# Differential attention in a two-layer block: scores on two row halves, one division less, nine steps beside the value products

## The chip, the cores and the metric

The program runs on one core of a Trainium2 chip. The metric is device time in microseconds for one execution: the median of three runs before the change. TensorE is called PE in the rows, VectorE DVE, ScalarE ACT, GpSimd POOL and SyncE SP; SP issues the transfers from HBM.

## The reference, cut to what matters

One transformer block of two layers is followed by a second one with a mixture of experts; the change touches the attention of the first block's second layer alone. There are 256 latent tokens and 256 context tokens, eight heads, and two components of 64 dimensions in each head:

```python
def diff_attn_core(q, k, v, lam):
    s = jnp.einsum('bqhcd,bkhcd->bhcqk', q, k) * DIFF_HEAD_DIM ** -0.5
    p = jax.nn.softmax(s, axis=-1)
    w = p[:, :, 0] - lam * p[:, :, 1]
    return jnp.einsum('bhqk,bkhe->bqhe', w, v)

def finish(o):
    o = rms_norm(o, subln_gain) * (1.0 - lam_init)
    return o.reshape(b, l, D_MODEL) @ w_out
```

Queries come from the 256 latent tokens, keys and values from all 512. Queries and keys are normalised by group of 64 and rotated before this.

## The kernel before, in words

`diff` first makes queries, keys and values with products of 128 by 128 by 512 in three passes (`mm3`, lines 142 to 144, on a high and a low part of each number). The loop `for i in range(3)` goes over queries, keys and values, `n` over the two halves of the 1024 columns, and `c` over four chunks of weights; a chunk for keys or values is 24 products, into `nj` = 4 accumulators that stay in PSUM for the whole of a half. After a half, ScalarE copies the four accumulators into `vt` (line 1213). `tick` between chunks runs what was put off: normalising, rotating, turning (`turn_qk`, line 1055) and placing the queries and keys. For the scores the queries lie in `qz` twice, with zeros in the rows of the other component, so that one product over 128 rows gives one component.

The attention itself is cut into 16 units u = 2 * head + half of the queries, and written out by hand as a pipeline of steps: `step(t)` issues the scores of unit t (line 1075), the turning of the weights of unit t - 3 (line 1100) with ScalarE's copy of it (line 1101), maxima and exponentials of unit t (lines 1080 and 1087), the weights of unit t - 2 on VectorE (lines 1092 to 1095) and the value products of unit t - 4 (line 1110). The tables `before` and `after` hang the outputs' work on steps: `o_evac` copies the outputs of a group of heads from PSUM, `o_norm` takes squares and the root, `o_scale` divides, `o_turn` (line 1137) turns, `o_split` makes a high and a low part, `out` multiplies by `diff_w_out`. Steps 0 to 3 stand behind the four chunks of the values' second half, the others follow by themselves.

Each engine runs its instructions in the order in which they are written. PSUM has eight buffers, all from one pool (`mm`): four for a half's accumulators, two for a unit's scores, one for a turned block, and in the later steps two for the outputs of a group. A new tile waits until the last reader of the buffer that it gets is done. Six buffers `raw` hold weights on their way in and, two units to a buffer, the exponentials.

Of the kernel before, what the change touches and what calls it, by code (L numbers as in the profile page):

```python
# [9 lines left out]
F32 = mybir.dt.float32  # L10
# [4 lines left out]
AF = mybir.ActivationFunctionType  # L15
OP = mybir.AluOpType
AX = mybir.AxisListType

P = 128
D = 1024  # L20
KD = D // P
L = 256
# [11 lines left out]
EPS = 1e-6  # L34
# [57 lines left out]
class Prog:  # L92
# [791 lines left out]
    def rest(self, cvec):  # L884
        nc, a = self.nc, self.a
# [10 lines left out]
        hh, hl, nx = self.first_norm  # L896

        def first(q):
# [7 lines left out]
        res = lambda layer, piece: lambda k, ps, c: self.add_res(  # L906
            k, ps, ((lat, self.md(layer, 0, piece)),) + (((ctxs, self.md(0, 1, piece)),) if layer == 0 else ()), c)


        lam = self.cp.tile([P, 4], F32, name="lam")  # L910
        subln = self.cp.tile([P, 1], F32, name="subln")
        tabs, norms = [], []
# [48 lines left out]


        kt = self.big([P, KD, T2], F32, "kt")
        qz = self.big([P, KD, 2, L], F32, "qz")
        nc.gpsimd.memset(qz[64:128, :, 0], 0.0)
        nc.gpsimd.memset(qz[0:64, :, 1], 0.0)
        vt = self.big([P, 4, D], F32, "vt")
        hn = self.diff(norms[0], norms[1], kt, qz, vt, tabs[0], tabs[1], lam, subln, res(1, 2))


        self.later(60, self.second_consts)
# [3 lines left out]
        hn = self.hn2 = self.big([P, 2, KD, L], FR, "hn")  # L975
# [35 lines left out]
        nrm.rstd()  # L1011
        nrm.apply()

    def diff(self, hh, hl, kt, qz, vt, tab, gr, lam, subln, res):
        nc, tc = self.nc, self.tc
        w_in = self.a["diff_w_in"]
        qst = self.cp.tile([P, 12, 8], F32, name="qst")
        st = self.cp.tile([P, 16, 8], F32, name="st")
        self.ints = st.rearrange("p a b -> p (a b)").bitcast(I32)
        so = self.so = self.cp.tile([P, 3, 8], F32, name="so")  # L1020
        def stage(n, j):
            return vt[:, j, n * 512:n * 512 + 512]

        def norm(q, n, j):

            r = qst[:, (0, 4)[q] + n * (2, 4)[q] + j]
            x = stage(n, j)
            x8 = x.rearrange("p (g d) -> p g d", g=8)
            sq = self.w(512, "sq")
            nc.scalar.activation(sq, x, AF.Square)  # L1030
            nc.vector.tensor_reduce(r[:, :, None], sq.rearrange("p (g d) -> p g d", g=8), axis=AX.X, op=OP.add)
            nc.scalar.activation(r, r, AF.Sqrt, bias=self.eps, scale=1.0 / 64)
            nc.vector.reciprocal(r, r)
            nc.vector.tensor_tensor(x8, x8, r[:, :, None].to_broadcast([P, 8, 64]), op=OP.mult)
# [17 lines left out]
        def turn_qk(q, n, j):  # L1052
            pt = tp[q, n, j] = self.mm()
            for i in range(4):
                nc.tensor.transpose(pt[:, i * P:i * P + P], stage(n, j)[:, i * P:i * P + P], self.c["ident"])

        def place(q, n, j):
            p4 = tp[q, n, j].rearrange("p (h t) -> p h t", h=4)
            hs, js = slice(4 * n, 4 * n + 4), slice(j * P, j * P + P)
            if q == 1:  # L1060
                nc.scalar.copy(kt[:, hs, js], p4)
            else:
                nc.scalar.copy(qz[0:64, hs, 0, js], p4[0:64])
                nc.scalar.copy(qz[64:128, hs, 1, js], p4[64:128])

        A, po = {}, {}
        groups = ((0, 4), (4, 2), (6, 2))
# [3 lines left out]
        def scores(u):  # L1071
            h, qc = u // 2, u % 2
            A[u, "s"] = [self.mm(), self.mm()]
            for c in range(2):
                nc.tensor.matmul(A[u, "s"][c], qz[:, h, c, qc * P:qc * P + P], kt[:, h], start=True, stop=True)

        def exps(u):
            sm = st[:, u]
            for c in range(2):
                nc.vector.reduce_max(sm[:, c:c + 1], A[u, "s"][c], axis=AX.X)  # L1080
            nc.vector.tensor_scalar(sm[:, 0:2], sm[:, 0:2], -0.125, None, op0=OP.mult)
            if u % 2 == 0:
                A["pw"] = self.raw([P, 2, 2, 512])
            A[u, "p"] = [A["pw"][:, u % 2, c] for c in range(2)]
            A[u, "w"] = A[u, "p"][1]
            for c in range(2):
                nc.scalar.activation(A[u, "p"][c], A[u, "s"][c], AF.Exp, scale=0.125, bias=sm[:, c:c + 1], accum_out=sm[:, 2 + c:3 + c])

        def weights(u):
            sm = st[:, u]  # L1090
            p0, p1 = A[u, "p"]
            nc.vector.reciprocal(sm[:, 4:6], sm[:, 2:4])
            nc.vector.tensor_tensor(sm[:, 6:7], sm[:, 5:6], lam[:, 2:3], op=OP.mult)
            nc.vector.tensor_scalar(p1, p1, sm[:, 6:7], None, op0=OP.mult)
            nc.vector.scalar_tensor_tensor(p0, p0, sm[:, 4:5], p1, op0=OP.mult, op1=OP.add)

        def turn(u):
            pt = self.mm()
            for kc in range(4):
                nc.tensor.transpose(pt[:, kc * P:kc * P + P], A[u, "p"][0][:, kc * P:kc * P + P], self.c["ident"])  # L1100
            nc.scalar.copy(A[u, "w"], pt)

        def values(u):
            h, qc = u // 2, u % 2
            g = group[h]
            i = h - groups[g][0]
            if i == 0:
                po[g, qc] = self.mm()
            for kc in range(4):
                nc.tensor.matmul(po[g, qc][:, i * P:i * P + P], A[u, "w"][:, kc * P:kc * P + P], vt[:, kc, h * P:h * P + P],  # L1110
                                 start=(kc == 0), stop=(kc == 3))
# [4 lines left out]
            nc.scalar.copy(A[g, "o", qc], po[g, qc][:, :n * P])  # L1116

        def o_norm(g):
            n = groups[g][1]
            for qc in range(2):  # L1120
                for i in range(n):
                    nc.scalar.activation(self.junk[:, i * P:i * P + P], A[g, "o", qc][:, i * P:i * P + P], AF.Square,
                                         accum_out=so[:, g, n * qc + i:n * qc + i + 1])
            nc.scalar.activation(so[:, g, :2 * n], so[:, g, :2 * n], AF.Sqrt, bias=self.eps, scale=1.0 / P)

        def o_scale(g):
            n = groups[g][1]
# [36 lines left out]
        b = lambda t, f, *args: before.setdefault(t, []).append((f, args))  # L1164
        e = lambda t, f, *args: after.setdefault(t, []).append((f, args))
        for g, qc, t in ((0, 0, 15), (0, 1, 16), (1, 0, 19), (1, 1, 19)):
            b(t, o_turn, g, qc)
            e(t, o_split, g, qc)
        for g, t in ((0, 11), (1, 15), (2, 19)):
            for qc in range(2):  # L1170
                b(t + qc, o_evac, g, qc)
            e(t + 1, o_norm, g)
            e(t + (3, 2, 1)[g], o_scale, g)
        for t, k in ((16, 0), (17, 1), (18, 2), (19, 3), (20, 4), (20, 5)):
            if k == KD - 3:
                for f in (o_turn, o_split):
# [4 lines left out]
        def step(t):  # L1181
            for f, args in before.get(t, ()):
                f(*args)
            if t < 16:
                scores(t)
            if 0 <= t - 3 < 16:
                turn(t - 3)
            if t < 16:
                exps(t)
            if 0 <= t - 2 < 16:  # L1190
                weights(t - 2)
            if 0 <= t - 4 < 16:
                values(t - 4)
            for f, args in after.get(t, ()):
                f(*args)

        for i in range(3):
            nj = 2 if i == 0 else 4
            for n in range(2):
                pt = [self.mm() for _ in range(nj)]  # L1200
                for c in range(4):
                    wh, wl = self.take()
                    for k in range(2):
                        kk = 2 * c + k
                        s = slice(k * 512, k * 512 + 512)
                        for j in range(nj):
                            js = slice(j * P, j * P + P)
                            self.mm3(pt[j], hh[:, kk, js], hl[:, kk, js], wh[:, s], wl[:, s], kk == 0, kk == KD - 1)
                    self.tick()
                    if i + n == 3:  # L1210
                        step(c)
                for j in range(nj):
                    nc.scalar.copy(stage(n, j), pt[j])
                    if i < 2:
                        at_ = j if i or n else j + 4
                        for d, f in enumerate((norm, rotate, turn_qk, place)):
                            self.later(at_ + d + (2 if i == 0 and n == 1 else 0), f, i, n, j)
        for t in range(4, 21):
            step(t)
        hn = self.big([P, 2, KD, L], FR, "hn")  # L1220
        nrm = self.Norm(self, slice(0, L), self.md(1, 0, 4), self.md(1, 0, 3), hn[:, 0], hn[:, 1])
# [1044 lines left out]
```

## Time and profile before

| | |
|---|---|
| median of three runs | 1411.95 us (1410.03 to 1413.07) |
| profiled execution | 1415.4 us, its span 1413.5 |
| TensorE busy | 1379.9 us, 98% of the span |
| VectorE busy | 780.9 us, 55% |
| ScalarE busy | 535.7 us, 38% |
| GpSimd busy | 8.6 us |
| read from HBM | 372.44 MB, 264 GB/s over the span |
| attention steps on TensorE (line 1075) | first start 575.5, last start 638.0 us |

The span is the time from the first to the last instruction of the program in the profile. Busy shares are means over stages with different limits, so the stage around the change has to be read by itself. A row of TensorE is longer than the distance to the next one, since products follow each other in a pipeline; distances between starts are what a product costs.

### The profile page before, as it was taken

The numbers are of one execution on the slowest core, as the hardware profiler recorded it, in microseconds if no ns is written. First come the engines' busy times: TensorE is split into PE (matmuls) and PEld (weight loads), VectorE is DVE, ScalarE is ACT, GpSimd is POOL, SyncE is SP. The second block draws the span as 40 slices with busy tenths as digits, with TensorE's granted clock in tenths as the row PEclk, the third lists the DMA queues.
The fourth block names the chain that finished last, engine by engine and source line by source line (L and its number), as shares of the span: only waits on it lengthen the run. The fifth ranks groups of instructions, "written<-read, shape, count | busy, mean of one in ns | idle before, by whom it ended". The sixth has DMA issues, their size and how long they took to land. (4 is left out here: it accounts for less than half of the span.)

```text
span 1413.5 us, 20416 instructions
## 1 busy us (share of the span) xinstructions
PE 1379.9 (98%) x8130; PEld 1020.4 (72%) x8130; DVE 780.9 (55%) x1377; ACT 535.7 (38%) x940; POOL 8.6 (1%) x16
## 2 busy tenths in 40 slices
PE   7999999999999999999999999999999999999997
PEld 5789888888889888768899999999543443443442
DVE  5688987778875787496865455676221121121112
ACT  5735322223134555486554345864210111111112
POOL 0000000000001000000000000000000000000000
PEclk9999999999999999999999999999999999999998
DMA  9984754977885531015585544629899999999994
GB/s 365 344 299 151 255 191 144 369 267 267 313 290 169 179 119 60 0 61 179 194 284 179 182 138 150 238 90 398 350 415 422 421 421 421 421 420 422 421 421 179
DMA packets 131426, 374.84 MB, mean 265 GB/s; under 512 B 9457, under 2 KB 63489, under 8 KB 109185
## 3 DMA queue, kind: packets, MB, share of 16 engines
q1 hardware_dynamic: 131328, 373.51, 70.0%
q8 instruction: 65, 1.06, 0.3%
q14 instruction: 33, 0.26, 0.1%
HBM read 372.44 MB, written 1.05 MB: 264 GB/s over the span
## 5 line engine op out<-in xcount | busy, mean ns | idle before, releaser
L133 DVE TENSOR_TENSOR hl<-raw,hl 128x1024 fp32r<-128x1024 f32 (+1 forms) x207 | 250.3, 1218 | 164.3 <-ACT hl L132 164.2
L132 ACT CAST hl<-raw 128x1024 fp32r<-128x1024 f32 (+1 forms) x207 | 213.3, 1044 | 255.4 <-PE mm L144 225.3
L342 DVE SCALAR_TENSOR_TENSOR junk<-raw,cb 128x1024 bf16<-128x1024 f32 x144 | 175.9, 1221 | 2.2
L142 PE MATMUL mm<-hh,hl 128*128 128x512 f32 (+1 forms) x384 | 142.9, 372 | 0.0
L143 PE MATMUL mm<-hl__790,hl 128*128 128x512 f32 (+1 forms) x384 | 142.7, 372 | 0.0
L144 PE MATMUL mm<-hh,hl 128*128 128x512 f32 (+1 forms) x384 | 142.6, 371 | 0.0
L142 PE MATMUL mm<-hn,hl 128*128 128x256 f32 (+1 forms) x488 | 140.2, 287 | 1.1 <-ACT hn L438 1.1
L143 PE MATMUL mm<-hn,hl 128*128 128x256 f32 (+1 forms) x488 | 139.9, 287 | 0.1
L144 PE MATMUL mm<-hn,hl 128*128 128x256 f32 (+1 forms) x488 | 139.2, 285 | 0.0
L142 PE MATMUL mm<-hidh,hl 128*128 128x256 f32 (+1 forms) x400 | 127.1, 318 | 0.0
L143 PE MATMUL mm<-hidl,hl 128*128 128x256 f32 (+1 forms) x400 | 126.7, 317 | 0.0
L144 PE MATMUL mm<-hidh,hl 128*128 128x256 f32 (+1 forms) x400 | 126.7, 317 | 0.0
L1997 PE MATMUL mm<-pre,X 128*64 128x512 f32 x376 | 119.4, 598 | 1.3 <-DMA pre<-in_w_gate 1.3
L1997 PE MATMUL mm<-raw,X 128*64 128x512 f32 x264 | 110.0, 599 | 1.6 <-DMA raw<-in_w_gate 1.3
L142 PEld LDWEIGHTS mm<-hn,hl 128*128 128x128 f32 (+1 forms) x488 | 94.1, 193 | 2.2 <-ACT hn L438 1.3
L2039 DVE SCALAR_TENSOR_TENSOR junk<-mm,rw,x 128x512 f32<-128x512 f32 x29 | 21.8, 752 | 133.7 <-PE mm L2010 131.6
L143 PEld LDWEIGHTS mm<-hn,hl 128*128 128x128 f32 (+1 forms) x488 | 94.1, 193 | 0.9 <-DVE hn L440 0.3
L2112 DVE TENSOR_TENSOR x<-x,mm 128x512 f32<-128x512 f32 x14 | 9.6, 688 | 153.5 <-PE mm L1997 153.5
L144 PEld LDWEIGHTS mm<-hn,hl 128*128 128x128 f32 (+1 forms) x488 | 94.2, 193 | 0.2
L142 PEld LDWEIGHTS mm<-hh,hl 128*128 128x128 f32 x384 | 72.3, 188 | 13.0 <-issue 0.4
L143 PEld LDWEIGHTS mm<-hl__790,hl 128*128 128x128 f32 x384 | 72.3, 188 | 12.6
L144 PEld LDWEIGHTS mm<-hh,hl 128*128 128x128 f32 x384 | 72.3, 188 | 12.4
(449 smaller groups left out, 2498.5 us busy)
## 6 DMA issues: line engine op xcount, KB each, us to landing
raw<-in_adaT SPq DMA_DIRECT2D x56, 1024.0 KB, 6.3
raw<-in_ffn_w_in SPq DMA_DIRECT2D x44, 1024.0 KB, 7.5
pre<-in_w_gate SPq DMA_DIRECT2D x25, 1024.0 KB, 19.7
raw<-in_ffn_w_out SPq DMA_DIRECT2D x22, 1024.0 KB, 5.0
pre<-in_w_up SPq DMA_DIRECT2D x22, 1024.0 KB, 19.8
pre<-in_w_down SPq DMA_DIRECT2D x21, 1024.0 KB, 19.7
raw<-in_w_gate SPq DMA_DIRECT2D x17, 1024.0 KB, 19.7
hl<-in_w_down SPq DMA_DIRECT2D x17, 1024.0 KB, 19.7
```

What stands on the lines that cost most here:

```text
L132: nc.scalar.copy(hi, src)
L133: nc.vector.tensor_tensor(lo, src, hi.bitcast(F32), op=OP.subtract)
L142: nc.tensor.matmul(out, ah, bh, start=start, stop=False)
L143: nc.tensor.matmul(out, ah, bl, start=False, stop=False)
L144: nc.tensor.matmul(out, al, bh, start=False, stop=stop)
L342: nc.vector.scalar_tensor_tensor(self.junk, hold[u][:, j], 1.0, self.cb[layer, s], op0=OP.mult, op1=OP.mult, accum_out=self.mod[layer, s][ ...
L1997: nc.tensor.matmul(St["gu", i][64 * m:64 * m + 64], x_of(k)[:, p % 2 * 2 + (0 if alone(p) else m)], St["w"][m][:, k % 4], start=(k == 0), ...
L2039: nc.vector.scalar_tensor_tensor(k2(t), k2(St["y", n]), self.rw[:, p // 2 % 2, p % 2:p % 2 + 1], gb[:, 2 * n:2 * n + 2], op0=OP.mult, op1= ...
L2112: nc.vector.tensor_tensor(sb, sb, St["gu", 1], op=OP.mult)
```

## The change

Queries are kept once, in `qt`. A unit's scores are four products over 64 rows and 256 columns: component 0 on rows 0 to 63, component 1 on rows 64 to 127, each on its own buffer. The weights are left undivided by the first component's sum: the second component is scaled by lam * sum0 / sum1 and added, and the constant in the output's normalisation is scaled by sum0 squared in its place. The steps beside the products for the values are 0 to 8: step 0 behind the last chunk of the first half, then two behind each chunk of the second half. Value products start at step 9, two units a step until step 13. The copied blocks of the first four units go into the second half of `qt`. The squares of the outputs are one pass with a sum on VectorE, and the first group's outputs are taken at step 13.

```diff
-        qz = self.big([P, KD, 2, L], F32, "qz")
-        nc.gpsimd.memset(qz[64:128, :, 0], 0.0)
-        nc.gpsimd.memset(qz[0:64, :, 1], 0.0)
+        qt = self.big([P, 2, KD, L], F32, "qt")
...
-                nc.scalar.copy(qz[0:64, hs, 0, js], p4[0:64])
-                nc.scalar.copy(qz[64:128, hs, 1, js], p4[64:128])
+                nc.scalar.copy(qt[:, 0, hs, js], p4)
...
-            for c in range(2):
-                nc.tensor.matmul(A[u, "s"][c], qz[:, h, c, qc * P:qc * P + P], kt[:, h], start=True, stop=True)
+            for m in range(2):
+                for c in range(2):
+                    r = slice(64 * c, 64 * c + 64)
+                    ms = slice(m * 256, m * 256 + 256)
+                    nc.tensor.matmul(A[u, "s"][c][:, ms], qt[r, 0, h, qc * P:qc * P + P], kt[r, h, ms], start=True, stop=True)
...
-            A[u, "w"] = A[u, "p"][1]
+            A[u, "w"] = qt[:, 1].rearrange("p h t -> p (h t)")[:, u * 512:u * 512 + 512] if u < 4 else A[u, "p"][1]
...
-            nc.vector.reciprocal(sm[:, 4:6], sm[:, 2:4])
-            nc.vector.tensor_tensor(sm[:, 6:7], sm[:, 5:6], lam[:, 2:3], op=OP.mult)
-            nc.vector.tensor_scalar(p1, p1, sm[:, 6:7], None, op0=OP.mult)
-            nc.vector.scalar_tensor_tensor(p0, p0, sm[:, 4:5], p1, op0=OP.mult, op1=OP.add)
+            nc.vector.reciprocal(sm[:, 4:5], sm[:, 3:4])
+            nc.vector.scalar_tensor_tensor(sm[:, 6:7], sm[:, 4:5], lam[:, 2:3], sm[:, 2:3], op0=OP.mult, op1=OP.mult)
+            nc.vector.scalar_tensor_tensor(p0, p1, sm[:, 6:7], p0, op0=OP.mult, op1=OP.add)
...
             for qc in range(2):
-                for i in range(n):
-                    nc.scalar.activation(self.junk[:, i * P:i * P + P], A[g, "o", qc][:, i * P:i * P + P], AF.Square,
-                                         accum_out=so[:, g, n * qc + i:n * qc + i + 1])
-            nc.scalar.activation(so[:, g, :2 * n], so[:, g, :2 * n], AF.Sqrt, bias=self.eps, scale=1.0 / P)
+                sq = self.w(512, "sq")[:, :n * P]
+                nc.scalar.activation(sq, A[g, "o", qc], AF.Square)
+                r = so[:, g, n * qc:n * qc + n]
+                nc.vector.tensor_reduce(r[:, :, None], sq.rearrange("p (h e) -> p h e", h=n), axis=AX.X, op=OP.add)
+                s0 = st[:, 2 * h0 + qc:2 * h0 + qc + 2 * n - 1:2, 2]
+                e = oe[:, g, n * qc:n * qc + n]
+                nc.vector.scalar_tensor_tensor(e, s0, EPS, s0, op0=OP.mult, op1=OP.mult)
+                nc.vector.scalar_tensor_tensor(r, r, 1.0 / P, e, op0=OP.mult, op1=OP.add)
+            nc.scalar.activation(so[:, g, :2 * n], so[:, g, :2 * n], AF.Sqrt)
...
-        for g, t in ((0, 11), (1, 15), (2, 19)):
+        for g, t in ((0, 13), (1, 15), (2, 19)):
             for qc in range(2):
-                b(t + qc, o_evac, g, qc)
-            e(t + 1, o_norm, g)
-            e(t + (3, 2, 1)[g], o_scale, g)
+                b(t + (g and qc), o_evac, g, qc)
+            e(t + min(g, 1), o_norm, g)
+            e(t + (1, 2, 1)[g], o_scale, g)
...
-            if 0 <= t - 4 < 16:
-                values(t - 4)
+            for u in ((2 * t - 18, 2 * t - 17) if 9 <= t < 14 else (t - 4,) if 14 <= t < 20 else ()):
+                values(u)
...
-                    if i + n == 3:
-                        step(c)
+                    if i == 2:
+                        for t in ((), (), (), (0,), (1, 2), (3, 4), (5, 6), (7, 8))[4 * n + c]:
+                            step(t)
...
-        for t in range(4, 21):
+        for t in range(9, 21):
```

Three places show how the instructions stand. The first is ScalarE's order around the first step; line 1213 before and 1220 now is the copy of a half's four accumulators into `vt`, and the load fetches the table of the exponential. Before:

```order
L1213 COPY vt<-mm 128x512 [waits PE_49] x4
L132 CAST hl<-raw 128x1024 [waits DMAHW2_49]
L1061 COPY kt<-mm 128x4x128 [waits PE_49]
L1087 ACT_TABLE_LOAD
L1087 ACTIVATE raw,st<-mm,st 128x512 [waits DVE_49]
L1087 ACTIVATE raw,st<-mm,st 128x512
L132 CAST hl<-raw 128x1024
```

And now:

```order
L1031 ACTIVATE qst<-qst,eps 128x8 [waits DVE_49]
L1088 ACT_TABLE_LOAD [waits DVE_49]
L1088 ACTIVATE raw,st<-mm,st 128x512 [waits PE_49] x2
L1220 COPY vt<-mm 128x512 x4
L132 CAST hl<-raw 128x1024 [waits DMAHW2_49]
L1060 COPY kt<-mm 128x4x128
L1088 ACTIVATE raw,st<-mm,st 128x512 [waits DVE_49,PE_49]
```

The exponentials of step 0 stand ahead of the copies of the first half, where they stood behind the copies and a conversion of weights; the load of the table stands behind a wait for VectorE, where it waited for nothing.

The second place is TensorE's order behind the last chunk of the values' second half: scores (`mm` from `kt` and `qz`, now `qt`), turned weights (from the unit matrix in `cst`) and value products (from `vt`). Before:

```order
L142 MATMUL mm<-hl,hh 128x512
L143 MATMUL mm<-hl,hh 128x512
L144 MATMUL mm<-hl,hl__3564 128x512
L1075 MATMUL mm<-kt,qz 128x512 x2
L1100 MATMUL mm<-cst,raw 128x128 x4
L1075 MATMUL mm<-kt,qz 128x512 x2
L1100 MATMUL mm<-cst,raw 128x128 x4
L1110 MATMUL mm<-vt,raw 128x128 x4
```

And now:

```order
L142 MATMUL mm<-hl,hh 128x512
L143 MATMUL mm<-hl,hh 128x512
L144 MATMUL mm<-hl,hl__3564 128x512
L1076 MATMUL mm<-kt,qt 128x256 x4
L1100 MATMUL mm<-cst,raw 128x128 x4
L1076 MATMUL mm<-kt,qt 128x256 x4
L1100 MATMUL mm<-cst,raw 128x128 x4
L1076 MATMUL mm<-kt,qt 128x256 x4
L1100 MATMUL mm<-cst,raw 128x128 x4
L1110 MATMUL mm<-vt,qt 128x128 x8
```

Behind a chunk stood one step, and the first step after the last chunk had four value products; now two steps stand behind the chunk, and the first step after the last chunk has eight value products.

The third place is ScalarE's order around the outputs of the first four heads (`o` from PSUM, its squares, the root in `so`). Before:

```order
L1116 COPY o<-mm 128x512 [waits PE_49]
L1101 COPY raw<-mm 128x512 [waits DVE_49,PE_49]
L1087 ACTIVATE raw,st<-mm,st 128x512 [waits DVE_49]
L1087 ACTIVATE raw,st<-mm,st 128x512
L1116 COPY o<-mm 128x512 [waits PE_49]
L1101 COPY raw<-mm 128x512 [waits DVE_49,PE_49]
L1087 ACTIVATE raw,st<-mm,st 128x512 [waits DVE_49,Activation_49]
L1087 ACTIVATE raw,st<-mm,st 128x512
L1122 ACTIVATE junk,so<-o 128x128 [waits Activation_49]
L1122 ACTIVATE junk,so<-o 128x128 x3
L1122 ACTIVATE junk,so<-o 128x128 [waits Activation_49] x4
L1124 ACT_TABLE_LOAD
```

And now:

```order
L1116 COPY o<-mm 128x512 [waits PE_49] x2
L1101 COPY raw<-mm 128x512 [waits DVE_49,PE_49,Activation_49]
L1088 ACTIVATE raw,st<-mm,st 128x512 [waits DVE_49]
L1088 ACTIVATE raw,st<-mm,st 128x512
L1123 ACTIVATE sq<-o 128x512 [waits Activation_49] x2
L1130 ACT_TABLE_LOAD
L1130 ACTIVATE so<-so 128x8 [waits DVE_49]
L1101 COPY raw<-mm 128x512 [waits PE_49]
L1088 ACT_TABLE_LOAD
L1088 ACTIVATE raw,st<-mm,st 128x512 [waits DVE_49]
L1088 ACTIVATE raw,st<-mm,st 128x512
```

The two copies stood in two successive steps, with the squares and the root at the end of the second; now both copies, the squares and the root stand in one step.

## Rows read from the trace of the kernel before

**Rows 1.** Busy us by stretch: engines (instructions), granted clock, DMA share, GB/s.

```profile
680.00:720.00 40.00, 40.00 (x315) 39.92 (x315) 36.10 (x57) 22.81 (x34) 0.00 (x0) 0.94 0.88 287
920.00:950.00 30.00, 30.00 (x229) 27.93 (x229) 20.86 (x34) 22.57 (x53) 0.10 (x1) 1.00 0.31 107
1100.00:1200.00 100.00, 100.00 (x496) 38.28 (x496) 16.67 (x38) 13.24 (x26) 0.00 (x0) 1.00 1.01 421
```

**Rows 2.** TensorE in order of time, a steady step: start, us, instruction.

```profile
606.49 1.88 PE L1075 MATMUL mm<-kt,qz 128*128 128x512 f32 x4
608.21 0.60 PE L1100 MATMUL mm<-cst,raw 128*128 128x128 f32 x4
608.64 1.06 PE L1110 MATMUL mm<-vt,raw 128*128 128x128 f32 x8
609.53 1.88 PE L1075 MATMUL mm<-kt,qz 128*128 128x512 f32 x4
```

**Rows 3.** Groups by line, 437 to 690: busy us, mean ns, idle before.

```profile
L1080 DVE TENSOR_REDUCE st<-mm 128x1 f32<-128x512 f32 x32 | 21.7, 688 | 11.4 <-PE mm L1075 11.4
L1095 DVE SCALAR_TENSOR_TENSOR raw<-raw,st 128x512 f32<-128x512 f32 x16 | 12.0, 751 | 0.6
L1094 DVE TENSOR_SCALAR raw<-raw,st 128x512 f32<-128x512 f32 x16 | 7.8, 487 | 0.6
L1081 DVE TENSOR_SCALAR st<-st 128x2 f32<-128x2 f32 x16 | 2.7, 170 | 0.5
L1087 ACT ACTIVATE raw<-mm,st 128x512 f32<-128x512 f32 x32 | 21.8, 688 | 14.8 <-DVE st L1081 10.4 <-DVE st L1092 4.4
L1101 ACT COPY raw<-mm 128x512 f32<-128x512 f32 x16 | 9.4, 587 | 15.8 <-PE mm L1100 15.7
```

**Rows 4.** TensorE in order of time where it waits, with the releaser.

```profile
636.25 0.63 PE L1137 MATMUL mm<-cst,o 128*128 128x128 f32 x4 [1.49 <-DVE o L1131]
...
643.14 0.38 PE L142 MATMUL mm<-oh,hl 128*128 128x256 f32 x1 [0.37 <-ACT oh L1145]
644.66 0.39 PE L143 MATMUL mm<-oh,hl 128*128 128x256 f32 x1 [1.14 <-DVE oh L1146]
```

**Rows 5.** TensorE in order of time, products over 64 rows, 912 to 921.5.

```profile
914.11 1.14 PE L1371 MATMUL mm<-B,x 64*128 64x256 f32 x8
915.08 1.91 PE L1388 MATMUL mm<-B 64*128 64x128 f32 x16
916.92 0.39 PE L142 MATMUL mm<-hn,hl 128*128 128x256 f32 x1
917.14 0.28 PE L143 MATMUL mm<-hn,hl 128*128 128x256 f32 x1
917.26 0.27 PE L144 MATMUL mm<-hn,hl 128*128 128x256 f32 x1
...
919.97 1.13 PE L1371 MATMUL mm<-B,x 64*128 64x256 f32 x4
```

**Rows 6.** ScalarE in order of time, ahead of the first step.

```profile
571.42 1.28 ACT L1087 ACT_TABLE_LOAD   x1
```

**Rows 7.** TensorE in order of time, two products for the values.

```profile
597.10 0.39 PE L143 MATMUL mm<-hl,hh 128*128 128x512 f32 x1
597.33 0.39 PE L144 MATMUL mm<-hl,hl__3564 128*128 128x512 f32 x1
```

**Rows 8.** SyncE in order of time: loads of the output weights.

```profile
625.01 6.47 SPq L152 DMA_DIRECT2D raw<-in_diff_w_out  x2
```

**Rows 9.** TensorE's busy us (instructions) by stretch, granted clock, DMA share, GB/s.

```profile
640.00:645.00 5.00, 2.60 (x19) 1.00 0.63 210
...
675.00:680.00 5.00, 3.13 (x16) 0.82 0.00 0
680.00:685.00 5.00, 5.00 (x24) 0.50 0.01 3
685.00:690.00 5.00, 5.00 (x43) 1.00 0.69 220
```

More of the change, by code (lines that the diff above doesn't have):

```diff
@@ L963, in rest @@
         kt = self.big([P, KD, T2], F32, "kt")
-        qz = self.big([P, KD, 2, L], F32, "qz")
-        nc.gpsimd.memset(qz[64:128, :, 0], 0.0)
-        nc.gpsimd.memset(qz[0:64, :, 1], 0.0)
+        qt = self.big([P, 2, KD, L], F32, "qt")
         vt = self.big([P, 4, D], F32, "vt")
-        hn = self.diff(norms[0], norms[1], kt, qz, vt, tabs[0], tabs[1], lam, subln, res(1, 2))
+        hn = self.diff(norms[0], norms[1], kt, qt, vt, tabs[0], tabs[1], lam, subln, res(1, 2))
         self.later(60, self.second_consts)
@@ L1012, in out_proj, with diff @@
         nrm.apply()
-    def diff(self, hh, hl, kt, qz, vt, tab, gr, lam, subln, res):
+    def diff(self, hh, hl, kt, qt, vt, tab, gr, lam, subln, res):
         nc, tc = self.nc, self.tc
@@ L1020, in diff @@
         so = self.so = self.cp.tile([P, 3, 8], F32, name="so")
+        oe = self.cp.tile([P, 3, 8], F32, name="oe")
         def stage(n, j):
@@ L1118, in o_norm @@
         def o_norm(g):
-            n = groups[g][1]
+            h0, n = groups[g]
             for qc in range(2):
-                for i in range(n):
-                    nc.scalar.activation(self.junk[:, i * P:i * P + P], A[g, "o", qc][:, i * P:i * P + P], AF.Square,
-                                         accum_out=so[:, g, n * qc + i:n * qc + i + 1])
-            nc.scalar.activation(so[:, g, :2 * n], so[:, g, :2 * n], AF.Sqrt, bias=self.eps, scale=1.0 / P)
+                sq = self.w(512, "sq")[:, :n * P]
[7 more added lines that the diff above has]
+            nc.scalar.activation(so[:, g, :2 * n], so[:, g, :2 * n], AF.Sqrt)
         def o_scale(g):
```

## The prediction

> **What bounds the kernel now.** I read the busy time by stretches first. TensorE is busy in all of 680 to 720 us and still in all of 920 to 950; between 1100 and 1200 the transfers run at 421 GB/s with a DMA share of 1.01 [rows 1]. The expert weights of that last stretch go into buffers that earlier TensorE work frees, so I take a shift of the attention stage as passed on to the end one for one. The change lies ahead of all this, between 560 and 680 us.
>
> Inside the attention I read TensorE's instructions in order of time. In a steady step the scores start at 606.49, the turning at 608.21, the value products at 608.64 and the next scores at 609.53 [rows 2]: 1.72 + 0.43 + 0.89 = 3.05 us without a gap. By the durations of VectorE's rows a step there is two maxima, a negation, three small rows, a 487 ns multiplication and a 751 ns multiply-and-add, about 3.0 us when laid behind each other [rows 3]; TensorE and VectorE are level, and ScalarE has two exponentials of 0.69 with an estimated 0.2 for reading out a sum and a copy of 0.59, some 2.1. TensorE's waits in the stage are few: 1.49 us before the first turning of the outputs, then 0.37 and 1.14 ahead of the output products [rows 4].
>
> **The change, part by part.** *Scores on two halves.* Each unit now issues four products of 64 rows by 256 columns, in two row halves, instead of two of 128 by 512. The same shape stands later in this trace: eight records (four products, each recorded twice) on both halves take 1.14 us, and the next group starts 0.97 after their start; four records on one half take 1.13 [rows 5]. So the halves run beside each other here. Going back to full rows costs something: the first product after the group lasts 0.22 where the next lasts 0.12, and I add 0.1 to 0.2 for emptying the array on either side. A unit then takes about 1.26 instead of 1.72: 16 x 0.46 = 7.4 us less. The bounds: no overlap would be about 1.9 (4.2 us more in all), no price of the change of shape 0.86 (13.8 less). I take 1.26, since rows 5 hold the very shape.
>
> The Trainium skill, "TensorEngine Tiling (Array Packing)", Theoretical Speedup, gives up to 2x for 64 rows; its Key Properties say that a change of tiling mode drains the engine. By the first alone the scores would give back the 13.8 us; the trace agrees with both, 1.13 for half the work beside 1.14, and 0.22 for 0.12 afterwards.
>
> *The division.* VectorE loses the 487 ns row [rows 3] and a step there falls to about 2.5 us. TensorE is busy in the steps from 9 to 13 (1.26 + 0.43 + 2 x 0.89 = 3.5 us), which hides it: 0. Were it not hidden it would be worth 0.5 a step.
>
> *Step 0 moves ahead of the second half of the value products.* The second half takes four accumulators out of eight PSUM buffers; the first half holds four until ScalarE has copied them, and now step 0's scores and the turned keys hold the rest. ScalarE's order shows the exponentials of step 0 ahead of these copies, and the table load behind a wait for VectorE. Before, the load ran at 571.42, long before it was needed [rows 6]; now it starts when the maxima are done. From the end of the scores: two maxima and the negation 1.55, load 1.28, first exponential with readout 0.85, together 3.7 us; TensorE has three products to do, at 0.23 each [rows 7]. **+3.0 us.**
>
> *Two steps a chunk.* Behind a first step's scores the second step's scores need two more buffers, and four are held by the accumulators. They come free from an exponential (1.55 + 0.85 = 2.4 us after the scores) or from the copy of a turned block (0.43 + 0.2 + 0.6 us); the second turning of a chunk waits for weights that VectorE makes behind the first step's maxima. Less what TensorE does meanwhile I get 2.3 us idle for steps 1 and 2, 1.7 for 3 and 4, 1.2 for 5 and 6 and for 7 and 8, and 0.6 at step 9, where the last accumulators are still held. **+7.0 us.** Nothing covers it, since TensorE runs its queue in order and the next 24 products stand behind. Before, one step a chunk had the chunk's 24 products, 5.5 us, for this.
>
> The Trainium skill's same page, PSUM Bottleneck, says that tiling speeds up TensorE but not the evacuation of PSUM. That speaks against this change; whether it decides here no row of the kernel before can show.
>
> *The outputs of the first four heads* are now taken at step 13 instead of 11 and 12, and turned at step 15 as before. From the start of step 13's scores: scores and maxima to 2.75, exponentials 4.2, two squares (by the exponentials' row) 5.6, sums and the root (with its table load) 7.0, while VectorE does the maxima of step 14 and the weights of 12 until 9.1, then reciprocal, scaling and the way to TensorE: 10.1. TensorE has 6.1 us of work until then (two steps of scores and turning, three sets of value products). It waits 4.0 instead of 1.49 [rows 4]. **+2.5 us.** The remaining waits are about the same; the first steps' two waits of 0.4 go: -0.9 with rounding.
>
> *Hidden.* One copy of the turned queries instead of two, beside products that keep TensorE busy: 0; uncovered, four copies would give some 0.6 each [rows 3]. The two memsets go from GpSimd, for which nothing in the stage waits. On the queue of SyncE the last two loads of the output weights wait for buffers that hold attention weights; they are issued from 625.01, and the first product that needs such weights starts at 643.14 [rows 4, 8]. The value products that free these buffers now run two a step and come no later against the output products: 0; late, they would cost what they are late.
>
> Sum: -7.4 + 3.0 + 7.0 + 2.5 - 0.9 = **+4.2 us**.
>
> *The clock.* After 675 to 680, in which TensorE was busy 3.1 of 5 us with only short products, the granted clock fell to 1.2 GHz; in the next 5 us it ran 24 products, and then 43 in 5 at 2.4 GHz [rows 9]: over 2 us lost in 5, some 3 in all. A stretch with 2.6 of 5 busy (640 to 645) was not followed by a fall. The new waits of 3 and 4 us lie between. A fall after the first costs about 3 us, since products stand behind; after the second 1 to 2, as other waits follow. I add 2 for it.
>
> The sum is made on the profiled execution, 1415.4 us (span 1413.5), which is 3.4 above the median; the difference of +6 applies to either. On the median of 1411.95: **1418 us**.
>
> **The rivals.** *The waits come without a fall of the clock*: 1411.95 + 4.2 = 1416. For it: the 640 to 645 row. Chance 0.24.
>
> *The change of shape costs nothing,* so a unit takes 0.86. Beside the value products, ScalarE and VectorE set the pace and give nothing back; the seven steps from 9 on gain 0.4 each, 2.8: 1411.95 + 4.2 - 2.8 = 1413.4, no change that can be measured (0.2%, 2.8 us, is about what a measurement of this kernel tells from none). Against it: the 0.22. Chance 0.20, with other ways in which the waits come out a few us shorter. The Trainium skill, "TensorEngine Tiling (Array Packing)", Theoretical Speedup, taken alone, would have it this way.
>
> *The second scores of a chunk find their buffers free,* because the buffer that comes round next is one whose reader was done long before. Then of the 7.0 some 1 is left, and the sum is -1.8; with the wait at the first turning back at 1.5 it is -4.3, 1407.7. It decides when the waits of the pairs stay under 3 us in all. Against it: four accumulators, two scores, a turned block and two scores are nine on eight buffers. Chance 0.11.
>
> *The halves do not overlap:* 1.9 a unit, 1411.95 + 4.2 + 7.4 + 4.2 = 1428. Rows 5 speak against it. Chance 0.04.
>
> **How the numbers follow.** The likeliest is the sum with one fall of the clock, chance 0.41, 1418 (its own range 1415 to 1422). Slower by over 0.2%: 0.41 + 0.24 + 0.04 = 0.69; within: 0.20; faster: 0.11. The range of 1409.5 to 1424 leaves out most of the faster case below, and above it the case without overlap and two falls together.
>
> **What the changed profile would show.** Score groups of about 1.1 us, pairs of products starting together. A TensorE wait of about 3 us behind step 0, put down to an exponential; a table load between step 0's maxima and its first exponential; waits of 1 to 2.5 us in front of the scores of steps 2, 4, 6 and 8; about 4 us in front of the first turning of the outputs, released by the scaling on VectorE. The first product of the second layer's feed-forward would stand 3 to 9 us later than before. I am wrong if the score groups take 1.7 or more, if the pairs show no wait, or if the clock stays up and the first output turning waits under 2 us.

## The result, and the profile after

The changed kernel takes 1420.65 us (median of seven executions, 1414.72 to 1422.36) against 1411.95 for the kernel before (1410.03 to 1413.07): a ratio of 1.0055 with a 95% interval of 1.0041 to 1.0068, so it is slower by 0.4 to 0.7%. The forecast was 1418 in a range of 1409.5 to 1424. The span of the profiled execution is 1418.8 us.

TensorE in order of time in the changed kernel; a number in brackets is the idle time ahead of a row and what ended it. Line 1076 is now the scores, 1054 the turned keys, 1143 the turning of the outputs.

```profile
567.09 0.60 PE L1054 MATMUL mm<-cst,vt 128*128 128x128 f32 x4
567.61 1.13 PE L1076 MATMUL mm<-kt,qt 64*128 64x256 f32 x8
568.68 0.50 PE L142 MATMUL mm<-hl,hh 128*128 128x512 f32 x1
569.01 0.40 PE L143 MATMUL mm<-hl,hh 128*128 128x512 f32 x1
569.25 0.39 PE L144 MATMUL mm<-hl,hl__3564 128*128 128x512 f32 x1
...
572.47 0.50 PE L142 MATMUL mm<-hl,hh 128*128 128x512 f32 x1 [2.83 <-ACT raw L1088]
...
577.90 1.56 PE L1076 MATMUL mm<-kt,qt 64*128 64x256 f32 x10
581.49 2.07 PE L1076 MATMUL mm<-kt,qt 64*128 64x256 f32 x6 [2.02 <-ACT raw L1088]
583.48 0.79 PE L142 MATMUL mm<-hl,hh 128*128 128x512 f32 x1
584.08 0.63 PE L143 MATMUL mm<-hl,hh 128*128 128x512 f32 x1
584.50 0.63 PE L144 MATMUL mm<-hl,hl__3564 128*128 128x512 f32 x1
...
594.18 0.70 PE L1076 MATMUL mm<-kt,qt 64*128 64x256 f32 x2 [0.67 <-ACT qt L1101]
595.30 1.13 PE L1076 MATMUL mm<-kt,qt 64*128 64x256 f32 x6 [0.43 <-ACT raw L1088]
...
604.09 1.87 PE L1076 MATMUL mm<-kt,qt 64*128 64x256 f32 x8
606.34 0.63 PE L1100 MATMUL mm<-cst,raw 128*128 128x128 f32 x4 [0.39 <-DVE raw L1095]
...
614.04 1.92 PE L1076 MATMUL mm<-kt,qt 64*128 64x256 f32 x8
616.30 0.63 PE L1100 MATMUL mm<-cst,raw 128*128 128x128 f32 x4 [0.34 <-DVE raw L1095]
616.85 1.92 PE L1076 MATMUL mm<-kt,qt 64*128 64x256 f32 x8
618.80 0.63 PE L1100 MATMUL mm<-cst,raw 128*128 128x128 f32 x4
...
621.15 1.14 PE L1076 MATMUL mm<-kt,qt 64*128 64x256 f32 x8
...
624.59 1.13 PE L1076 MATMUL mm<-kt,qt 64*128 64x256 f32 x8
...
641.46 0.63 PE L1143 MATMUL mm<-cst,o 128*128 128x128 f32 x4 [3.94 <-DVE o L1137]
...
649.58 0.39 PE L143 MATMUL mm<-oh,hl 128*128 128x256 f32 x1 [0.78 <-DVE oh L1152]
```

Four things are to be seen. A unit's scores (eight records, four products) take 1.07 us to the next start, where [rows 2] had 1.72, and the first product behind them is 0.33 from the next instead of 0.23. Behind step 0 TensorE waits 2.83 us for an exponential (line 1088). Behind the scores of a chunk's first step it waits for the second's buffers: 2.02 us at 581.49; 0.67 and 0.43 at 594; and 1.18 at 604.09, where the group is 2.25 from the next start and 1.07 of that is work. (A wait that is shorter than the pipelined end of the row ahead stands inside a group without brackets. The group at 614.04 has another 1.19 and the one at 616.85, step 9, another 0.88, by the same subtraction. The 0.39 and 0.34 in brackets at 606.34 and 616.30 are part of these sums; there TensorE waits for VectorE's weights and not for a buffer. What stands inside the three groups ends when ScalarE's copy of a turned block, line 1101, has freed a buffer: the trace puts the weight loads that go with these products down to it.) And in front of the first turning of the outputs it waits 3.94 us where it waited 1.49 [rows 4].

The fifth is the clock. From 584.08 a product is 0.42 us from the next instead of 0.23. The same stretches in the table of busy time, whose PEclk column (third from the end) is the granted clock as a share of 2.4 GHz:

```profile
570.00:575.00 5.00, 2.53 (x11) 2.06 (x12) 0.23 (x2) 4.64 (x10) 0.00 (x0) 1.00 0.00 0
575.00:580.00 5.00, 4.46 (x26) 3.31 (x24) 2.76 (x4) 1.46 (x3) 0.00 (x0) 1.00 0.20 29
580.00:585.00 5.00, 3.52 (x10) 2.39 (x11) 2.52 (x8) 1.84 (x5) 0.00 (x0) 0.64 0.45 180
585.00:590.00 5.00, 5.00 (x17) 3.99 (x16) 1.82 (x2) 2.47 (x6) 0.00 (x0) 0.68 0.00 0
...
640.00:645.00 5.00, 3.54 (x20) 2.81 (x21) 3.42 (x9) 2.26 (x7) 0.00 (x0) 0.78 0.00 2
645.00:650.00 5.00, 3.81 (x26) 3.42 (x25) 3.85 (x10) 4.98 (x12) 0.00 (x0) 0.88 0.51 162
```

TensorE ran at 1.2 GHz for part of 580 to 590, behind the wait at 581, and for part of 640 to 650, behind the wait at the outputs. Before, nothing between 560 and 675 ran below 1.00.

ScalarE around step 0 shows why the first wait is as long as it is:

```profile
570.35 1.28 ACT L1088 ACT_TABLE_LOAD   x1 [6.38 <-DVE st L1082]
571.64 0.69 ACT L1088 ACTIVATE raw<-mm,st 128x512 f32<-128x512 f32 x1
```

ScalarE had been idle for 6.38 us and began the load only when VectorE had written the maxima; before, the load was done long ahead of its use [rows 6].

**How the runs are compared below.** Profiles start up to 2 us apart, so each is measured from the first turned keys of the 567 to 570 region (567.09 above, 569.18 before) to the second product of the output projection (649.58 above, 644.66 in [rows 4]). That stretch is 75.48 us before and 82.49 after: +7.0 us. This number of a single profile tells tenths where a timed median tells one or two us.

| kernel | stretch, us | against before | timed ratio, 95% interval |
|---|---|---|---|
| before | 75.48 | | |
| changed | 82.49 | +7.0 | 1.0055 (1.0041 to 1.0068) |
| changed, once more | 83.27 | +7.8 | 1.0052 (1.0034 to 1.0069) |
| row halves alone | 74.72 | -0.8 | 0.9989 (0.9980 to 0.9998) |
| undivided weights alone | 75.85 | +0.4 | 1.0000 (0.9990 to 1.0011) |
| changed, steps of before | 72.93 | -2.6 | 0.9986 (0.9978 to 0.9995) |
| changed, early table | 81.21 | +5.7 | 1.0038 (1.0024 to 1.0051) |
| changed, steps apart | 75.73 | +0.3 | 1.0009 (0.9999 to 1.0018) |
| changed, outputs earlier | 83.41 | +7.9 | not timed |
| changed, filled wait | 79.16 | +3.7 | not timed |
| the same, once more | 83.90 | +8.4 | 1.0062 (1.0045 to 1.0079) |
| eight steps apart | 71.94 | -3.5 | 0.9974 (0.9960 to 0.9988) |
| the same, values spread | 68.70 | -6.8 | 0.9959 (0.9943 to 0.9974) |

### The profile page after: what moved, and what is told of

Read it like the earlier page. It is cut to its first block, busy times and chain, and to the rows that moved or that the text cites. A ratio compares the mean times of both kernels' runs of the same rounds, so it can differ in the third digit from the quotient of the medians.

```text
span 1418.8 us, 20501 instructions
## 1 busy us (share of the span) xinstructions
PE 1378.1 (97%) x8194; PEld 1024.2 (72%) x8194; DVE 777.6 (55%) x1379; ACT 530.1 (37%) x910; POOL 5.0 (0%) x14
```

## The experiments

**Row halves alone.** The kernel before with this part of the change only:

```diff
-        qz = self.big([P, KD, 2, L], F32, "qz")
...
+        qt = self.big([P, 2, KD, L], F32, "qt")
...
+            for m in range(2):
+                for c in range(2):
...
+                    nc.tensor.matmul(A[u, "s"][c][:, ms], qt[r, 0, h, qc * P:qc * P + P], kt[r, h, ms], start=True, stop=True)
```

> The kernel before with the scores on two row halves and queries kept once, nothing else of the change. Theory: from the fifth unit on TensorE and VectorE are level at 3.05 and 3.0 us a step before, so with VectorE as it was only the four units beside the products gain, 0.55 each, and the others 0.05: about 2.5 us faster, 1409.5. Rival, TensorE sets the pace alone: 16 x 0.55 = 8.8 us faster, 1403.

Measured 1410.76 us, 0.9989 (0.9980 to 0.9998): a little faster, near the first theory. TensorE in order of time, two steps:

```profile
607.77 1.13 PE L1075 MATMUL mm<-kt,qt 64*128 64x256 f32 x8
609.29 0.63 PE L1100 MATMUL mm<-cst,raw 128*128 128x128 f32 x4 [0.39 <-DVE raw L1095]
...
610.74 1.13 PE L1075 MATMUL mm<-kt,qt 64*128 64x256 f32 x8
```

A step is 2.97 us, not 2.5: what the scores save, TensorE waits for VectorE's weights. The faster scores are taken back by an engine that was level with TensorE. The stretch gained 0.8, of the 2.5 expected; part of the rest went to the clock behind 631 to 634, where TensorE waited 0.70 and 1.33 us and the next scores' records took 2.08 instead of 1.13.

**Undivided weights alone.** The kernel before with the new `weights` and `o_norm`:

```diff
-            nc.vector.tensor_scalar(p1, p1, sm[:, 6:7], None, op0=OP.mult)
-            nc.vector.scalar_tensor_tensor(p0, p0, sm[:, 4:5], p1, op0=OP.mult, op1=OP.add)
+            nc.vector.scalar_tensor_tensor(p0, p1, sm[:, 6:7], p0, op0=OP.mult, op1=OP.add)
```

> The kernel before with the weights left undivided (and the sums of squares as in the change), scores and steps as before. Theory: TensorE's 3.05 us a step stay, VectorE's shorter step buys nothing: within 0.2% of 1412. Rival, VectorE sets the pace: 12 steps of 0.5 us, 6 us faster, 1406.

Measured 1412.79, 1.0000 (0.9990 to 1.0011). TensorE's 3.05 us a step hide the shorter row. The run holds the new sums of squares too, and these are not free: at the outputs TensorE waits 1.38 us for weights and 1.82 for the scaling, where before it waited 0.41 and 1.49. So what the shorter row may give outside the steady steps is not told apart from them.

**Both, with the steps of before.** The changed kernel with the loop, the values, the tables and the place of the copied blocks of before (only the loop is shown):

```diff
-                    if i == 2:
-                        for t in ((), (), (), (0,), (1, 2), (3, 4), (5, 6), (7, 8))[4 * n + c]:
-                            step(t)
+                    if i + n == 3:
+                        step(c)
```

> The changed kernel with the steps, the value products and the outputs at the places of the kernel before: row halves and undivided weights stay. Theory: the loss of the change is the nine steps beside the products alone; here TensorE and VectorE both need 2.5 us a step, so four units gain 0.55 and twelve 0.5, some 8 us faster than before, less up to 2 at the outputs: 1404 to 1406. Rival, the row halves or the undivided weights carry a cost of their own or the waits move to VectorE: not below 1410.

Measured 1410.31, 0.9986 (0.9978 to 0.9995): faster than before, and 10 us below the change, so the loss lies in the new places of the steps and of what hangs on them. But it gained 2.6 us in the stretch and not 8, and the rival's 1410 is nearer than the theory's 1404. A step falls to 2.68 us on average (2.55 and 2.81 in turn), and then the outputs of the first four heads break the pace. VectorE, in order of time:

```profile
624.85 0.69 DVE L1125 TENSOR_REDUCE so<-sq 128x4 f32<-128x512 f32 x1 [0.93 <-ACT sq L1123]
...
626.59 1.28 DVE L1081 TENSOR_REDUCE st<-mm 128x1 f32<-128x512 f32 x2
```

and TensorE:

```profile
629.32 0.63 PE L1100 MATMUL mm<-cst,raw 128*128 128x128 f32 x4 [2.67 <-DVE raw L1095]
...
633.68 2.08 PE L1076 MATMUL mm<-kt,qt 64*128 64x256 f32 x8
```

VectorE waits 0.93 us for the squares and sums for 1.7 us (624.85 to 626.59), with the next maxima and weights queued behind; TensorE, level with it, waits 2.67 us for the weights, and the scores behind run at the low clock (2.08 us for eight records instead of 1.13).

**The table loaded early.** The changed kernel with one column's exponential ahead of step 0:

```diff
+            if t == 0:
+                nc.scalar.activation(self.junk[:, :1], self.eps, AF.Exp)
             if t < 16:
                 scores(t)
```

> The changed kernel with one exponential of a single column at the start of step 0, so that the table is loaded ahead of the wait for the maxima. Theory: the wait behind step 0 falls from 2.83 to about 1.5 us, 1.3 us faster than the change if the clock does the same as there: 1419.3. Rival, the wait is that for the copies of the accumulators and not for the exponential: 2.8 us stay and 1420.6.

The wait behind step 0 is 1.56 us instead of 2.83, and the stretch 1.3 shorter. Timed it is 1417.5, 1.0038 (1.0024 to 1.0051); that interval overlaps the change's, and the 1.27 us are read from the trace. The first theory holds: the load was in the way.

**Steps apart.** The changed kernel with the first step of each pair in the middle of its chunk:

```diff
+                        if k == 0 and i + n == 3:
+                            step(2 * c + 1)
...
-                        for t in ((), (), (), (0,), (1, 2), (3, 4), (5, 6), (7, 8))[4 * n + c]:
+                        for t in ((), (), (), (0,), (2,), (4,), (6,), (8,))[4 * n + c]:
```

> The changed kernel with the first step of each pair moved into the middle of its chunk (after 12 of the 24 products), so that no two steps stand back to back; step 0 and all behind step 8 unchanged. Theory: the 5.5 us of waits within the pairs come from the second scores finding no free buffer; 12 products (2.75 us) between two steps free them, the pair waits fall to under 1 us in all and the fall of the clock at 583 goes too: 7 to 8 us less than the change up to step 9, time about 1413. Rival, the steps wait for weights and exponentials that are late whatever stands between: 1 to 2 us less, 1419.

Measured 1413.35, 1.0009 (0.9999 to 1.0018), as the theory said. Of the sums of TensorE's waits from 565 to 645:

```profile
PE mm L1143 <- DVE o L1137: 3.9, 1, 3.9
PE mm L142 <- ACT raw L1088: 2.8, 1, 2.8
...
PE mm L1100 <- DVE raw L1095: 0.3, 1, 0.3
```

No bracketed wait of scores (line 1076) is left. By the subtraction used above 0.46 us remain at step 4 (1.53 us to the next start) and 1.19 at step 9, which still stands right behind step 8:

```profile
609.86 1.92 PE L1076 MATMUL mm<-kt,qt 64*128 64x256 f32 x8
612.12 0.63 PE L1100 MATMUL mm<-cst,raw 128*128 128x128 f32 x4 [0.34 <-DVE raw L1095]
```

So of the 6.4 us of waits at the second steps and at step 9, 4.7 are gone with the standing back to back; the number of steps beside the products is the same nine. The stretch is 6.8 us shorter. The rest of that is in the main the clock: it was below 1.00 in 570 to 580 (0.92 and 0.74, behind step 0) and 635 to 640 (0.66), which is less than in the change. What stays besides are the waits behind step 0 and at the outputs.

**Outputs earlier.** The changed kernel with the first four heads' outputs copied, squared and rooted at the end of step 12:

```diff
-        for g, t in ((0, 13), (1, 15), (2, 19)):
+        for g, t in ((0, 12), (1, 15), (2, 19)):
             for qc in range(2):
-                b(t + (g and qc), o_evac, g, qc)
+                (b if g else e)(t + (g and qc), o_evac, g, qc)
```

> The changed kernel with the outputs of the first four heads copied, squared and rooted at the end of step 12 and divided at the end of 13, a step earlier. Theory: the 3.94 us in front of the first turning of the outputs fall under 1, and with them the slow clock behind; the output products start 3 to 5 us earlier than in the change. Rival: the work on ScalarE and VectorE is only pushed onto the exponentials of step 13, and a wait of 3 to 4 us stands ahead of the turned weights instead.

One execution, 1420.7, without an interval. The wait of 3.94 is gone and 2.1 us stand in front of turned weights instead, put down to the reciprocal of the root on VectorE, with 0.9 behind it: mostly the rival. From the turned weights of step 8 (618.13, in the change 616.30) to the second output product it is 32.68 us instead of 33.28, so 0.6 were won; the stretch as a whole is longer, since the clock was low behind step 0 as well.

**A filled wait.** The changed kernel with TensorE busy in most of the wait at the outputs; the value products of step 14 are done four times, which is work for nothing:

```diff
-                values(u)
+                for _ in range(4 if t == 14 else 1):
+                    values(u)
```

> The changed kernel with the value products of step 14 issued four times over (each time from the start, so the last leaves the same sums): 2.8 us of TensorE work in front of the wait for the first turning of the outputs. Theory: the turning starts when it did, the wait falls from 3.94 to about 1.1 us, the clock stays at 2.4 GHz behind it, and the output products start about 1.4 us earlier than in the change. Rival, the slow products behind it are no matter of the idle time: they stay slow, and the output products start when they did.

One execution, 1418.43. The wait is 1.27 us, and the clock stays at 1.00 behind it. But it also stayed at 1.00 between 580 and 590, where this kernel is the changed kernel, instruction by instruction. So three kernels more were run on one chip: the change again, the filled one again, and the last one below.

> The changed kernel once more, beside the two below. Both theories: 1420 to 1421. If the slow clock behind the waits is a matter of the execution and not of the code, the stretches at 1.2 GHz stand at other waits in this profile than in the first (there at 582 to 588 and 642 to 646).

> The kernel with the value products of step 14 four times over, now timed. Theory: the filled wait never slows the clock, so behind the first turning of the outputs it is at 2.4 GHz in this profile too, and the median is about 1.4 us below that of the changed kernel. Rival, the first profile had the full clock there by chance: the median is that of the changed kernel, within 0.5 us.

The change again: 1419.77, 1.0052 (1.0034 to 1.0069). The filled kernel: 1420.6, 1.0062 (1.0045 to 1.0079). The filled kernel is 0.8 us the slower of the two, with intervals that overlap: no gain, as the rival said, but not for the rival's reason. In the change run again the low clock stands behind step 0, where the first profile had none, and at the two other waits. Busy time by stretch, of the change again:

```profile
570.00:575.00 5.00, 2.17 (x13) 1.27 (x12) 1.46 (x3) 2.53 (x4) 0.00 (x0) 1.00 0.00 0
575.00:580.00 5.00, 5.00 (x17) 3.88 (x16) 1.83 (x2) 3.57 (x8) 0.00 (x0) 0.66 0.00 0
...
585.00:590.00 5.00, 4.78 (x16) 3.60 (x17) 2.50 (x7) 3.26 (x10) 0.00 (x0) 0.66 0.00 0
...
645.00:650.00 5.00, 4.81 (x31) 3.86 (x30) 2.60 (x7) 2.66 (x8) 0.00 (x0) 0.74 0.05 16
```

of the filled kernel's first profile:

```profile
580.00:585.00 5.00, 3.12 (x15) 2.38 (x16) 3.19 (x9) 2.20 (x7) 0.00 (x0) 1.00 0.48 197
585.00:590.00 5.00, 5.00 (x29) 3.90 (x27) 1.46 (x2) 2.12 (x5) 0.00 (x0) 1.00 0.00 0
...
645.00:650.00 5.00, 3.74 (x29) 3.54 (x30) 3.69 (x10) 3.41 (x6) 0.00 (x0) 1.00 0.33 112
```

and of its second:

```profile
575.00:580.00 5.00, 5.00 (x23) 3.94 (x23) 1.83 (x2) 1.80 (x3) 0.00 (x0) 0.85 0.16 12
...
585.00:590.00 5.00, 5.00 (x13) 3.61 (x12) 3.32 (x7) 2.87 (x6) 0.00 (x0) 0.50 0.00 0
...
645.00:650.00 5.00, 3.56 (x30) 3.11 (x28) 3.68 (x10) 3.90 (x10) 0.00 (x0) 1.00 0.43 134
```

The filled wait kept the clock up in both profiles, so that half of the theory held. But there was little to win. From the first turning of the outputs to the second output product it is 8.12 us in the change and 8.83 when run again, 7.89 in both profiles of the filled kernel: 0.2 to 0.9 us, not 1.4, because at the full clock 0.86 us of waiting for weights come back. The earlier waits decide much more, and they go by the execution: of one and the same program up to 616 us (the outputs-earlier kernel is the same until then) one profile had no slow stretch there, one had one and three had two.

**Eight steps apart.** Eight steps beside the products, none of them behind the first half's last chunk, values two a step from step 8 and the first outputs a step earlier:

```diff
+                        if k == 0 and i + n == 3:
+                            step(2 * c)
...
+                        for t in ((), (), (), (), (1,), (3,), (5,), (7,))[4 * n + c]:
...
+            for u in ((2 * t - 16, 2 * t - 15) if 8 <= t < 12 else (t - 4,) if 12 <= t < 20 else ()):
...
-        for g, t in ((0, 13), (1, 15), (2, 19)):
+        for g, t in ((0, 12), (1, 15), (2, 19)):
```

> The changed kernel with eight steps beside the products, in the middle and at the end of each chunk of the second half (step 0 in the middle of the first of them), the value products two a step from step 8 to 11 and the outputs of the first four heads a step earlier. Theory: no wait behind step 0, none in pairs, under 1 us at the outputs, no fall of the clock before 670: 9 to 11 us less up to the output products than before's loss of 7.0 in the change, some 8 to 9 us less than the change, 1403 to 1409 in the end. Rival, the row halves and undivided weights give nothing even so: 1412 or more.

Measured 1408.62, 0.9974 (0.9960 to 0.9988): faster than before and within the expected times, though the stretch gained 3.5 us and not more, since 2.7 us of waiting for VectorE stood at the outputs of the first heads, with a slow clock behind it (0.88 and 0.78 in 625 to 635).

**Values spread.** The same, with value products left for the steps in which VectorE does the outputs:

```diff
-            for u in ((2 * t - 16, 2 * t - 15) if 8 <= t < 12 else (t - 4,) if 12 <= t < 20 else ()):
+            for u in {8: (0,), 9: (1, 2), 10: (3, 4), 11: (5,), 12: (6, 7), 13: (8, 9), 14: (10,), 15: (11,), 16: (12,), 17: (13,), 18: (14,), 19: (15,)}.get(t, ()):
...
+        b(13, o_evac, 0, 0)
+        b(13, o_evac, 0, 1)
+        b(13, o_square, 0)
+        e(13, o_norm, 0)
+        e(13, o_scale, 0)
+        b(15, o_turn, 0, 0)
```

> The kernel with eight steps apart, and besides the value products spread (one unit in steps 8 and 11, two in 9, 10, 12 and 13), the outputs of the first four heads copied and squared at the start of step 13, summed and divided at its end, turned in step 15. Theory: the 2.67 us in front of the turned weights come from VectorE, which waits for the squares and the root with the next maxima behind it; two value units in steps 12 and 13 give TensorE 1.9 us more to do there, the waits between step 8 and the output products fall from 4.6 to about 2.5 us, and the output products start 2 us earlier: 1405 to 1407. Rival, VectorE's work for the outputs is too long for any place, and the wait only moves: 1408 to 1409.

Measured 1405.28, 0.9959 (0.9943 to 0.9974): the fastest kernel here, 6 us below before and 15 below the change. TensorE's waits, 565 to 640:

```profile
PE mm L1100 <- DVE raw L1095: 2.4, 4, 1.0
PE mm L1149 <- DVE o L1143: 0.8, 1, 0.8
PE mm L143 <- DVE oh L1158: 0.5, 1, 0.5
PE mm L1076 <- ACT raw L1088: 0.3, 1, 0.3
```

No wait is over 1 us, and no stretch up to the output products ran at the low clock. The waits behind step 8 sum to 3.3 us and not 2.5 (with eight steps apart, by the same count, 5.3), and the output products start 3 us earlier than with eight steps apart, not 2; the slow stretch went too. The places of the value products and of the outputs were changed together, so the run does not tell which of the two did it.

## Why the prediction was right, and which term was off

The time lay in the range, and the mechanism was the one forecast, with the clock dearer than it was put: the scores on row halves give back what was said, and the steps put back to back, the table load and the outputs take more. Step by step:

- *Scores, 7.4 us.* Right. From the turned keys ahead of step 0 to the third product behind its scores it is 2.16 us (567.09 to 569.25). Before it was 2.62:

```profile
575.10 0.60 PE L1055 MATMUL mm<-cst,vt 128*128 128x128 f32 x4
...
577.72 0.39 PE L144 MATMUL mm<-hl,hl__3564 128*128 128x512 f32 x1
```

  That is 0.46 for a unit, the number forecast. A later step with eight value products (621.15 to 624.59) takes 3.44 where 3.5 was forecast. A group alone is shorter than the 1.26 forecast (1.07), and the products around it pay the change of shape, about 0.1 on either side.
- *The division, 0.* Right for the steady steps, by the run with undivided weights alone (3.05 us a step as before). With faster scores as well it is worth something: row halves alone step at 2.97 us, both together at 2.68.
- *Step 0, +3.0.* 2.83. The early table halves it to 1.56; that part is the load, and the rest is the maxima and the exponential.
- *Two steps a chunk, +7.0.* 2.02 + 1.10 + 1.18 + 1.19 + 0.88 = 6.4 us, where 2.3, 1.7, 1.2, 1.2 and 0.6 were forecast. Some 0.7 of it is for VectorE's weights, the rest for buffers that were still being read. The steps apart show that it is the standing back to back: the same nine steps have 1.7 us of it. The Trainium skill, "TensorEngine Tiling (Array Packing)", PSUM Bottleneck, says that tiling speeds up TensorE but not the evacuation of PSUM; the trace agrees in so far as 7.4 us were won on the scores and some 5.6 lost to such buffers, though with another order of the steps most of the loss goes.
- *The outputs, +2.5.* 3.94 against 1.49: +2.45.
- *The sum, +4.2.* At the full clock it is +3.7: the first profile of the filled kernel, which ran at 2.4 GHz throughout the stretch.
- *The clock, +2.* This is the term that was mis-sized. The two profiles of the change have +7.0 and +7.8, so the clock cost 3.3 and 4.1 us, and 4.7 in the second profile of the filled kernel. I had taken one fall, behind the first wait or at the outputs. But [rows 9] hold one stretch behind which the clock fell and one, with more idle time, behind which it did not, so they gave no ground for one fall rather than two or three. The clock falls behind the 2.02 us wait inside the first pair too, which I had not counted, and there dense products stand behind it: in the first profile the ten that start from 583.48 to 587.49 are 0.42 us apart or more instead of 0.23. Up to the turned weights at 616 us the change needed 3.1 us more than the filled kernel's first profile (49.21 from the first turned keys, there 46.11), with the same instructions and one slow stretch more. At the outputs the fall costs 0.2 to 0.9, less than the 1 to 2 that I gave it.

The 1418 came out 2.7 us too low. In the stage the pairs that were put 0.6 too high made up for a part of the clock that was put 1.3 to 2.1 too low, so the nearness of the sum is in part luck.

A shift of the stage is passed on about one for one: +7.0 and +7.8 in the stretch, 8.7 and 8.5 between the medians. From profile to profile the stage begins 2.1 us earlier in the change than before, its second output product starts 4.9 later and TensorE's last product 5.8 later (1404.07 before, 1409.90 now); for the change run again the two are 7.8 and 5.4. So 0.7 to 1.7 us between the medians are not settled. Later stretches fall to the low clock in some profiles and not in others (in that of the change 994 to 998 us at 0.57, which cost 1.6 and which before had at 1.00; the feed-forward's fall at 680 to 688 was 1.2 cheaper than [rows 9]), and single profiles do not tell whether that belongs to the change.

Of the rivals, buffers that are free are refuted (6.4 us of waits, where it had some 1), and so is no overlap (1.07 a group, where it had 1.9; its price was put too high, since 16 x 0.18 is 2.9 and not 4.2). That the change of shape costs nothing is refuted as well (1.07 for 0.86, and 0.33 for 0.23 behind a group). Waits without a fall of the clock, 1416, is what one profile of the stage in four shows, the first of the filled kernel; three of the thirteen timed executions of the change lie between 1414.5 and 1415.4 and the others between 1419.3 and 1422.4. The granted clock over the whole span, which is on record for every execution, is 0.994 in the three lower ones and 0.990 to 0.992 in the others; 0.002 to 0.004 of 1419 us is 3 to 6 us, which is most of the difference. So the lower ones lost less to the clock, though where they lost less is not shown, since they have no profile.

## What to carry to other kernels

When TensorE and VectorE are level, work taken from one alone buys next to nothing (0.9989 and 1.0000 here), from both at once no more than that with the old order of the steps (0.9986), and the gain comes out only when the schedule leaves neither waiting: the same two edits gave 1.0055, 0.9986 and 0.9959 with three orders of the steps. Before putting two pipeline steps back to back beside a long accumulation, count PSUM buffers over time: nine on eight, with the waits for weights beside them, cost 6.4 us, and half a chunk of products between the steps left 1.7. A wait of TensorE ahead of dense products can cost more in clock than in waiting (2.02 us waited, 3.1 lost behind it in one profile and nothing in another), and the fastest kernel here keeps TensorE work for the stretch in which another engine must catch up.

## What the runs showed of the hardware that was not expected

With the same program and the same wait the clock falls in one execution and not in another. Behind the 2.83 us wait after step 0 it was below 1.00 in four of six profiles, behind the 2.02 us wait of the first pair in five of six, behind the 3.9 us wait at the outputs in all four, and behind the 1.27 us that the filler left of it in neither of two. So these traces give no single price of a wait in clock: it was 0 to 4.7 us for this stage, and what decides between them no run here shows.

Two row halves with four products of 64 by 256 take 1.07 us, 0.62 of the two products over 128 rows that they replace [rows 2], and the first full-row product behind them 0.1 us more than the others.
